# Moving a LayerNorm's sums and seven subtractions' operands to the vector engine, and cutting the last two norms into three parts

## The chip, the cores and the metric

The kernel runs on one core of one Trainium2 chip. The time is device microseconds of one launch; three runs of the kernel before gave 2405.48, 2411.17 and 2411.96 us, median 2411.17 us. The engines in the text are PE (TensorE, matrix products), DVE (VectorE), ACT (ScalarE), POOL (GpSimd) and SP (SyncE, which issues most DMAs).

## The reference, cut to what matters

One layer of a streaming encoder over 1088 tokens (1024 of a prompt, 64 of a running stream), model width 1024, feed-forward width 2816. Everything up to the mixed branch output `m` (a gated linear recurrence and a differential attention) is left out here; the change lies behind it:

```python
h   = layer_norm(ALPHA * x + m @ w_out, ln1_g, ln1_b)      # 1024 wide, over the features of one token
up  = h @ w_up                                             # 1024 x 5632: 2816 values and 2816 gates
c   = conv_b + sum(conv_w[j] * shifted(up, j) for j in range(3))
val, gate = split(c)
out = layer_norm(ALPHA * h + (silu(gate) * val) @ w_down, ln2_g, ln2_b)

def layer_norm(x, g, b):
    mu  = mean(x); var = mean(square(x - mu))
    return (x - mu) * rsqrt(var + 1e-5) * g + b
```

## The kernel before

Tokens lie along the free dimension and features along the 128 partitions, so `h` is eight tiles `z[0..7]` of 128 features. The 1088 tokens are four quarters of 272. Set c=0 holds quarters 0 and 2, set c=1 quarters 1 and 3; h=0 and h=1 name the two quarters of a set.

Every product is computed in three passes of single-pass float32 matmuls: each operand is split into a rounded part (hi, a cast on ACT) and the rest (lo, a subtraction on DVE), and hi*hi, hi*lo and lo*hi are summed in PSUM. `load_w` loads weights in tiles of 128x512 and splits them the same way (lines 82 and 83, names `whi` and `wlo`); `split_tokens` (lines 116 and 117) splits the activations, 128x1088 at a time.

`mix` ends with `out(0)`, the norms of set 0, and `out(1)`: the product with `w_out`, whose sums DVE moves to `z` (line 994). `layer_norm` takes the mean over 1024 features with eight full float32 matmuls with a matrix of 1/1024 (line 761, for the last set; two instructions each), subtracts it on DVE (line 773), squares on ACT (777 and 780), adds the squares up in two sums (781: for the last set one sum on POOL, one on DVE), turns the sums with small matmuls into a variance per token on the partitions (785), adds epsilon on DVE (792), takes the power -1/2 on POOL (793), spreads it again by a scaled identity (797, DVE) and a matmul (798), and scales and shifts (801 on DVE, 802 on ACT). `norm` then stores the quarter by two DMAs of ACT's queue and splits it.

`ffn` begins at line 1096. The first two of 22 feature pairs (f=0 and f=1) use `plain` (line 1051): a product of 24 matmuls for each quarter and each of two rows (value and gate). `norm(1, 0)` and `norm(1, 1)` stand between these. The other 20 pairs use `seven_products` (line 155), a scheme with 7 instead of 8 block products of each set, which needs besides b11, b21 and b22 the four combinations t1 to t4 of the blocks; `seven_tokens` (`sums(c)`) makes these by subtractions of 128x1088 in place (lines 125, 128, 130 and 133, on POOL) and splits them. The combinations of the weights are made on POOL as well (line 99). `conv` does the convolution of one pair, mostly on DVE.

Work on each engine is in order. The order is set at build time by a list scheduler: it simulates the engines and takes of what is ready the instruction that comes first in the program, or that was given a higher priority. Tiles come from pools of a fixed number of buffers; `mb` for instance has two, which the two parts of b12 of set 0 hold until the `plain` products of set 0 are done, and those of set 1 take after that.

The core of `ffn` before the seven-product loop:

```python
self.norm(1, 0)
plain(0, u0, 0, (0, 1))       # f, u, set, quarters: 2 rows x 2 quarters x 24 matmuls
self.norm(1, 1)
plain(1, u1, 0, (0, 1))
...
plain(0, u0, 1, (0,))
plain(1, u1, 1, (0,))
self.sums(0)
plain(1, u1, 1, (1,))
plain(0, u0, 1, (1,))
self.sums(1)
```

Of the kernel before, what the change touches and what calls it, by code (L numbers as in the profile page):

```python
# [10 lines left out]
F32 = mybir.dt.float32  # L11
# [3 lines left out]
ALU = mybir.AluOpType  # L15
# [5 lines left out]
P = 128  # L21
D = 1024
KT = D // P
# [6 lines left out]
EPS = 1e-5  # L30
# [7 lines left out]
QW = T // 4  # L38
# [12 lines left out]
class K:  # L51
# [67 lines left out]

    def seven_tokens(self, out, z, tile):  # L120

        V, G = self.nc.vector, self.nc.gpsimd
        b11, b21, b12, b22 = (z[n] for n in ("b11", "b21", "b12", "b22"))
        t1 = b11
        G.tensor_tensor(t1, b12, b11, ALU.subtract)
        self.split_tokens(out, "t1", t1, tile)
        t3 = b12
        G.tensor_tensor(t3, b22, b12, ALU.subtract)
        t2 = b22
        G.tensor_tensor(t2, b22, t1, ALU.subtract)  # L130
        self.split_tokens(out, "t2", t2, tile)
        t4 = b21
        G.tensor_tensor(t4, b21, t2, ALU.subtract)
        self.split_tokens(out, "t3", t3, tile)
        self.split_tokens(out, "t4", t4, tile)

    def seven_products(self, lanes, tmp):

# [609 lines left out]
        return [([t[:, c0:c0 + cw] for t in hs], [t[:, c0:c0 + cw] for t in ls]) for c0, cw in QUARTERS]  # L748


    def layer_norm(self, z, cw, og, ob, pp, lp, last=False):

        nc = self.nc
        V, S, G = nc.vector, nc.scalar, nc.gpsimd

        def lt(tag, bufs):
            return lp.tile([P, cw], F32, tag=tag, name=self.nm(tag), bufs=bufs)
        mean = pp.tile([P, 512], F32, tag="mm", name=self.nm("mean"))
        if last:
            for j in range(KT):  # L760
                nc.tensor.matmul(mean[:, :cw], self.ones_d, z[j], start=(j == 0), stop=(j == KT - 1))
        else:
            acc = lt("acc", 2)
            V.tensor_tensor(acc, z[0], z[1], ALU.add)
            for j in range(2, KT):
                V.tensor_tensor(acc, acc, z[j], ALU.add)
            nc.tensor.matmul(mean[:, :cw], self.ones_d, acc, start=True, stop=True)

        blocks = [(b, min(P, cw - b)) for b in range(0, cw, P)]
        var = pp.tile([P, 512], F32, tag="mm", name=self.nm("var"))  # L770
        sums = [None, None]
        for j in range(KT):
            V.tensor_tensor(z[j], z[j], mean[:, :cw], ALU.subtract)
            i = j % 2 if last else 0
            if sums[i] is None:
                sums[i] = lt("acc", 2)
                S.activation(sums[i], z[j], AF.Square)
                continue
            sq = lt("sq", 3)
            S.activation(sq, z[j], AF.Square)  # L780
            (V if i else G).tensor_tensor(sums[i], sums[i], sq, ALU.add)
        sums = [x for x in sums if x is not None]
        for i, (b, n) in enumerate(blocks):
            for j, x in enumerate(sums):
                nc.tensor.matmul(var[:n, i:i + 1], x[:, b:b + n], self.ones_d[:, 0:1], start=(j == 0),
                                 stop=(j == len(sums) - 1))
        rs = lp.tile([P, 2, 3], F32, tag="rs", name=self.nm("rs"), bufs=2)
        rb = pp.tile([P, 512], F32, tag="mm", name=self.nm("rb"))
        full = cw // P
        for n, i0, i1 in ((P, 0, full), (cw % P, full, len(blocks))):  # L790
            if i0 < i1:
                V.tensor_scalar(rs[:n, 0, i0:i1], var[:n, i0:i1], EPS, None, ALU.add)
                G.tensor_tensor(rs[:n, 1, i0:i1], rs[:n, 0, i0:i1], self.mhalf[:n].to_broadcast([n, i1 - i0]),
                                ALU.pow)
        for i, (b, n) in enumerate(blocks):
            dg = lp.tile([P, P], F32, tag="dg", name=self.nm("dg"), bufs=2)
            V.tensor_scalar(dg[:n, :n], self.ident[:n, :n], rs[:n, 1, i:i + 1], None, ALU.mult)
            nc.tensor.matmul(rb[:, b:b + n], self.ones_1[:n, :], dg[:n, :n], start=True, stop=True)
        for j in range(KT):
            g, b = self.par[:, og + j:og + j + 1], self.par[:, ob + j:ob + j + 1]  # L800
            V.scalar_tensor_tensor(z[j], z[j], g, rb[:, :cw], ALU.mult, ALU.mult)
            S.activation(z[j], z[j], AF.Identity, bias=b)
# [133 lines left out]
    def mix(self):  # L936
        tc, nc, a, o = self.tc, self.nc, self.a, self.o
        V, S, G = nc.vector, nc.scalar, nc.gpsimd
        mm, lnp = self.mm, self.lnp
# [3 lines left out]
        lp = ms.enter_context(tc.tile_pool(name="lp", bufs=2, **right))  # L943
# [7 lines left out]
        def m1t(name, dt=F32R):  # L951
            return m1.tile([P, 4, QW], dt, tag="mc", name=self.nm(name), bufs=16)
# [21 lines left out]
        def m2t(name, dt=F32R, tag="mc"):  # L974
            return m2.tile([P, 4, QW], dt, tag=tag, name=self.nm(name), bufs=12 if tag == "mc" else 2)
# [4 lines left out]
        lp = self.lx.enter_context(tc.tile_pool(name="ln", bufs=2, **right))  # L980
# [4 lines left out]
        def out(c):  # L985
            for j in range(KT):
                w = self.load_w(self.wcols(a["w_out"][0], j * P))
                for h, q in enumerate(pairs[c]):
                    c0 = q * QW
                    ps = self.proj_chunk(mm, w, [mh[q][k // 4][:, k % 4, :] for k in range(KT)],  # L990
                                         [ml[q][k // 4][:, k % 4, :] for k in range(KT)], QW)
                    xr = small("g")
                    nc.sync.dma_start(xr, self.s_x[j * P:(j + 1) * P, c0:c0 + QW])
                    V.scalar_tensor_tensor(zs[c][f"b{1 + j // 4}{1 + h}"][:, j % 4, :], xr, ALPHA, ps,
                                           ALU.mult, ALU.add)

        def norm(c, h):

            c0 = pairs[c][h] * QW
            names = [f"b{1 + i}{1 + h}" for i in range(2)]  # L1000
            z = [zs[c][n] for n in names]
            self.layer_norm([z[k // 4][:, k % 4, :] for k in range(KT)], QW, self.o_l1g, self.o_l1b, lnp, lp, c == 1)
            for i in range(2):
                S.dma_start(self.s_r.rearrange("(i k p) t -> i p k t", i=2, p=P)[i, :, :, c0:c0 + QW], z[i])
                self.split_tokens(self.xop[c], names[i], z[i],
                                  lambda n: m2t(n, tag="mb") if names[i] == "b12" else m1t(n))
# [4 lines left out]
        self.norm, self.sums = norm, sums  # L1011
        out(0)
        for h in range(2):
            norm(0, h)
        out(1)

    def ffn(self):
        tc, nc, a, o = self.tc, self.nc, self.a, self.o
        V, S, G = nc.vector, nc.scalar, nc.gpsimd
# [5 lines left out]
        mm, lnp = self.mm, self.lnp  # L1025
# [16 lines left out]
        def put(u, c):  # L1042
            def f(row, half):
                t0 = (2 * half + c) * QW
                for s0, s1, off in ((0, TP, 2), (TP, T, 4)):
                    b, e = max(s0, t0), min(s1, t0 + QW)
                    if b < e:
                        yield slice(b - t0, e - t0), u[:, row, b + off:e + off]
            return f

        def plain(f, u, c, halves, rows=(0, 1)):

            for row in rows:
                w = self.load_w(self.wcols(a["w_up"][0], (f + row * NF) * P))
                for h in halves:
                    x = self.xop[c][f"b1{1 + h}"] + self.xop[c][f"b2{1 + h}"]
                    ps = self.proj_chunk(mm, w, [k[0] for k in x], [k[1] for k in x], QW)
                    for sl, dst in put(u, c)(row, h):
                        S.copy(dst, ps[:, sl])
# [28 lines left out]


        u0, u1 = us = [new_u(f) for f in range(2)]  # L1090
        self.norm(1, 0)
        plain(0, u0, 0, (0, 1))
        self.norm(1, 1)
        plain(1, u1, 0, (0, 1))
        self.lx.close()
        cp = self.ux.enter_context(tc.tile_pool(name="upc", bufs=1, side="right", reuse_waits="tile"))
        plain(0, u0, 1, (0,))
        plain(1, u1, 1, (0,))
        self.sums(0)
        plain(1, u1, 1, (1,))  # L1100
# [24 lines left out]
        for ci, (c0, cw) in enumerate(DCH):  # L1125
# [16 lines left out]
            for j in range(KT):  # L1142
                ps = mm.tile([P, 512], F32, tag="mm", name=self.nm("mm"))
                for g0, gn in ((0, 8), (8, 8), (16, 6)):
                    src = wd[g0 * P:(g0 + gn) * P, j * P:(j + 1) * P].rearrange("(k p) c -> p k c", p=P)
                    w = self.load_w(src, gn)
                    for k in range(gn):
                        f = g0 + k
                        hi, lo = w[k]
                        for i, (l, r) in enumerate(((hi, ah), (hi, al), (lo, ah))):  # L1150
                            nc.tensor.matmul(ps[:, :cw], l, r[f][:, :cw], start=(f == 0 and i == 0),  # L1151
                                             stop=(f == NF - 1 and i == 2))
                hr = ft.tile([P, DW], F32, tag="hr", name=self.nm("hr"), bufs=2)
                nc.sync.dma_start(hr[:, :cw], self.s_r[j * P:(j + 1) * P, c0:c0 + cw])
                z = ft.tile([P, DW], F32, tag="z", name=self.nm("z2"), bufs=2)
# [6 lines left out]
            for i, (r, n) in enumerate(rows):  # L1162
# [3 lines left out]
                sq = ft.tile([P, D], F32, tag="sq", name=self.nm("sq"), bufs=1)  # L1166
# [7 lines left out]
                k = min(n, TP - t0)  # L1174
# [38 lines left out]
```

## Time and profile before

| what | value |
|---|---|
| median of 3 runs | 2411.17 us (2405.48 to 2411.96) |
| profiled execution, own time | 2406.6 us |
| its span in the trace | 2404.8 us |
| mean granted TensorE clock | 0.992 |
| PE busy | 2345.5 us, 98% |
| DVE busy | 1546.2 us, 64% |
| ACT busy | 1103.3 us, 46% |
| POOL busy | 549.1 us, 23% |

Times in the profile are microseconds from the start of the span. Busy time of an engine leaves out its waits. A timeline row gives start, duration, engine, line, operation, the tile written and the tiles read, how many instructions of the same kind follow one another, and in brackets how long the engine stood idle before it and what ended that. The granted clock is a share of full speed.

### The profile page before, as it was taken

The page shows a single profiled execution, that of the slowest core. Times are in us where ns is not written, and L with a number is a line of the kernel's source. Part 1 is how long each engine was busy: PE and PEld are TensorE (multiplying, and loading weights), DVE is VectorE, ACT ScalarE, POOL GpSimd, SP SyncE. Part 2 cuts the span into 40 slices and gives each one's busy share as a digit, 9 for nine tenths or more (in the row PEclk, how much of TensorE's full clock was granted, in tenths as well). Part 3 has the DMA queues.
Part 4 walks back from the last instruction along what each step waited for, and adds up shares of the span by engine and source line. Part 5 has one row for each costly group of instructions (what it writes and reads, how often), then busy time and mean ns, then how long its engine had stood idle before and what let it go on. Part 6 is the DMA issues. An engine that isn't in the chain of part 4 may idle for free.

```text
span 2404.8 us, 42987 instructions
## 1 busy us (share of the span) xinstructions
PE 2345.5 (98%) x16534; PEld 2289.3 (95%) x16534; DVE 1546.2 (64%) x2672; ACT 1103.3 (46%) x2134; POOL 549.1 (23%) x594
## 2 busy tenths in 40 slices
PE   8999999999999999999999999998999999989997
PEld 8999999999999999999999999998999999989997
DVE  3666665554666565565557565578978777766764
ACT  3444444443344444444447543245444444456664
POOL 2222222222521121121120000144544444200100
PEclk9999999999999999999999999998999999999999
DMA  4111111112622332332336674444332233298865
GB/s 128 39 40 47 42 44 49 40 35 65 200 81 79 108 90 73 98 99 74 96 92 199 200 243 136 131 140 125 104 94 82 85 94 95 84 268 252 241 202 150
DMA packets 404580, 273.02 MB, mean 114 GB/s; under 512 B 21803, under 2 KB 393927, under 8 KB 404374
## 3 DMA queue, kind: packets, MB, share of 16 engines
q1 hardware_dynamic: 399638, 265.52, 37.3%
q10 hardware_dynamic: 4224, 4.46, 0.6%
q8 instruction: 130, 2.13, 0.4%
q0 software_dynamic: 512, 0.29, 0.1%
q14 instruction: 76, 0.62, 0.1%
HBM read 199.65 MB, written 57.96 MB: 107 GB/s over the span
## 4 chain that ended last, share of the span: by engine, by line
PE 89%; DMA 3%; DVE 3%; ACT 2%; issue 1%; POOL 0%; SPq 0%; POOLq 0%; DVEq 0%; ACTq 0%
PE mm L182 46%; PE mm L155 18%; PE mm L1151 11%; PE s L645 3%; PE av L686 2%; PE wt L680 1%; PE lv L408 1%; PE nat L334 1%; DMA gb<-s_g 1%; PE o L491 1%; DVE wlo L83 1%; DMA ydl<-s_yd 1%; PE o L494 1%; PE avd L731 1%; PE bs L441 1%
## 5 line engine op out<-in xcount | busy, mean ns | idle before, releaser
L182 PE MATMUL mm<-x,whi 128*128 128x362 f32 (+1 forms) x3456 | 876.5, 333 | 5.0 <-ACT x L312 3.7
L182 PEld LDWEIGHTS mm<-x,whi 128*128 128x128 f32 x3456 | 611.7, 189 | 10.8 <-ACT x L312 4.4
L182 PE MATMUL mm<-x,wlo 128*128 128x362 f32 (+1 forms) x1728 | 573.2, 332 | 0.0
L83 DVE TENSOR_TENSOR wlo<-wraw,whi 128x512 fp32r<-128x512 f32 x516 | 377.0, 736 | 267.0 <-ACT whi L82 257.3
L82 ACT CAST whi<-wraw 128x512 fp32r<-128x512 f32 x516 | 308.5, 605 | 439.3 <-PE mm L182 211.5
L182 PEld LDWEIGHTS mm<-x,wlo 128*128 128x128 f32 x1728 | 326.7, 189 | 1.7 <-issue 1.0
L1151 PE MATMUL mm<-ah,whi 128*128 128x288 f32 (+1 forms) x688 | 200.3, 292 | 2.1 <-ACT ah L1135 2.1
L1151 PE MATMUL mm<-al,whi 128*128 128x288 f32 (+1 forms) x688 | 200.1, 291 | 1.5 <-DVE al L1136 1.5
L1151 PE MATMUL mm<-ah,wlo 128*128 128x288 f32 (+1 forms) x688 | 200.2, 292 | 0.0
L1151 PEld LDWEIGHTS mm<-ah,whi 128*128 128x128 f32 x688 | 131.2, 191 | 2.6 <-ACT ah L1135 2.4
L1151 PEld LDWEIGHTS mm<-al,whi 128*128 128x128 f32 x688 | 130.8, 190 | 1.9 <-DVE al L1136 1.9
L1151 PEld LDWEIGHTS mm<-ah,wlo 128*128 128x128 f32 x688 | 130.6, 190 | 1.0 <-DVE wlo L83 0.9
L536 POOL TENSOR_TENSOR rs<-rs,mhalf 128x4 f32<-128x4 f32 (+1 forms) x24 | 22.0, 919 | 372.7 <-DVE rs L535 372.7
L572 POOL TENSOR_TENSOR KL<-kT,B 64x512 fp32r<-64x512 f32 x32 | 49.2, 1539 | 218.1 <-DVE B L571 193.5
L82 ACT CAST whi<-wsum 128x512 fp32r<-128x512 f32 x80 | 49.6, 620 | 89.2 <-PE mm L155 84.2
L645 PE MATMUL s<-B,A 128*128 128x512 f32 (+3 forms) x384 | 87.7, 354 | 2.1 <-ACT E L666 1.6
L388 POOL TENSOR_TENSOR P<-X,k 128x544 f32<-128x544 f32 (+1 forms) x32 | 60.3, 1884 | 122.8 <-ACT X L382 68.7
L169 DVE TENSOR_TENSOR u<-mm,p 128x272 f32<-128x272 f32 (+2 forms) x160 | 55.1, 366 | 49.7 <-PE mm L155 49.7
L681 ACT COPY wT<-wt 128x512 f32<-128x512 f32 (+1 forms) x96 | 46.3, 482 | 80.1 <-PE wt L680 79.5
L99 POOL TENSOR_TENSOR wsum<-wraw,wraw 128x512 f32<-128x512 f32 x40 | 72.6, 1814 | 45.6 <-DVE wlo L83 45.5
L686 PE MATMUL av<-dvn,wT 128*128 128x128 f32 x576 | 80.0, 275 | 0.1
L1074 DVE SCALAR_TENSOR_TENSOR c<-u,par,c 128x1090 f32<-128x1090 f32 x44 | 78.4, 1782 | 0.3 <-ACT c L1071 0.3
(382 smaller groups left out, 5918.5 us busy)
## 6 DMA issues: line engine op xcount, KB each, us to landing
wraw<-w_down SPq DMA_DIRECT2D x160, 256.0 KB, 3.6
wraw<-w_in SPq DMA_DIRECT2D x144, 256.0 KB, 2.9
wraw<-w_up SPq DMA_DIRECT2D x124, 256.0 KB, 3.1
wraw<-w_br_hg SPq DMA_DIRECT2D x48, 256.0 KB, 4.1
s_act<-c SPq DMA_DIRECT2D x22, 512.0 KB, 3.1
A<-A SPq DMA_DIRECT2D x64, 128.0 KB, 2.6
wraw<-w_out SPq DMA_DIRECT2D x32, 256.0 KB, 2.9
araw<-s_act SPq DMA_DIRECT2D x44, 144.0 KB, 4.0
```

The source lines that it names most:

```text
L82: nc.scalar.copy(hi[:, :kn, :], raw[:, :kn, :])
L83: nc.vector.tensor_tensor(lo[:, :kn, :], raw[:, :kn, :], hi[:, :kn, :].bitcast(F32), ALU.subtract)
L99: G.tensor_tensor(t, x, y, op)
L155: nc.tensor.matmul(ps, l, r, start=(first and k == 0 and i == 0), stop=(k == 3 and i == 2), skip_group_check=not first)
L169: V.tensor_tensor(dst, ps[:, sl], d[other][:, sl], ALU.add)
L182: nc.tensor.matmul(ps[:, :cw], l, r[:, :cw], start=(k == 0 and i == 0), stop=(k == n - 1 and i == 2))
L388: G.tensor_tensor(pk, xv[:, :, :hb], blocks(k, B)[:, :, :hb], ALU.mult)
L572: G.tensor_tensor(kl[r], kT[r, sl], b[r, m, :].bitcast(F32), ALU.subtract)
L645: nc.tensor.matmul(dst[:, kc * 512:kc * 512 + kw], A[i // 2][:, p, m, qc], B[kc][:, m, :kw], start=(p == 0), stop=(p == 1))
L686: self.last_av = nc.tensor.matmul(av[:, i % n4, :], wT[:, kb, :], vn[:, kb, :], start=(kb == 0), stop=(kb == i))
L1074: V.scalar_tensor_tensor(t[:, :W - 2], u[:, i, 1:W - 1], par[:, self.o_w1 + j:self.o_w1 + j + 1], t[:, :W - 2], ALU.mult, ALU.add)
L1151: nc.tensor.matmul(ps[:, :cw], l, r[f][:, :cw], start=(f == 0 and i == 0), stop=(f == NF - 1 and i == 2))
```

## The change

1. `seven_tokens` makes t1 to t4 on DVE instead of POOL.
2. In the last set's norms all sums of squares are on DVE (before: alternating POOL and DVE). Norms of set 0 keep theirs on POOL.
3. The 272 columns are taken as three blocks of 128, the third (from column 144) overlapping the second, where before the third had 16. So epsilon and the power are one instruction each for all three, not two. `dg` has three buffers instead of two.
4. `layer_norm` and `norm` become generators with two stops: after the mean's matmuls, and after the variance's. `ffn` calls both last norms up to the first stop ahead of all `plain` products, and the other parts between single rows of these. The second norm's mean takes its PSUM bank from the pool `mm` of six.
5. The mean's matmuls (last set), the variance's, and all from epsilon to the spreading matmul get a priority 2000 instructions ahead of their place.

```diff
--- before.py
+++ after.py
@@ -119,20 +119,16 @@
 
     def seven_tokens(self, out, z, tile):
 
-        V, G = self.nc.vector, self.nc.gpsimd
+        V = self.nc.vector
         b11, b21, b12, b22 = (z[n] for n in ("b11", "b21", "b12", "b22"))
-        t1 = b11
-        G.tensor_tensor(t1, b12, b11, ALU.subtract)
-        self.split_tokens(out, "t1", t1, tile)
-        t3 = b12
-        G.tensor_tensor(t3, b22, b12, ALU.subtract)
-        t2 = b22
-        G.tensor_tensor(t2, b22, t1, ALU.subtract)
-        self.split_tokens(out, "t2", t2, tile)
-        t4 = b21
-        G.tensor_tensor(t4, b21, t2, ALU.subtract)
-        self.split_tokens(out, "t3", t3, tile)
-        self.split_tokens(out, "t4", t4, tile)
+        V.tensor_tensor(b11, b12, b11, ALU.subtract)
+        self.split_tokens(out, "t1", b11, tile)
+        V.tensor_tensor(b12, b22, b12, ALU.subtract)
+        V.tensor_tensor(b22, b22, b11, ALU.subtract)
+        self.split_tokens(out, "t2", b22, tile)
+        V.tensor_tensor(b21, b21, b22, ALU.subtract)
+        self.split_tokens(out, "t3", b12, tile)
+        self.split_tokens(out, "t4", b21, tile)
 
     def seven_products(self, lanes, tmp):
 
@@ -748,25 +744,31 @@
         return [([t[:, c0:c0 + cw] for t in hs], [t[:, c0:c0 + cw] for t in ls]) for c0, cw in QUARTERS]
 
 
-    def layer_norm(self, z, cw, og, ob, pp, lp, last=False):
+    def layer_norm(self, z, cw, og, ob, pp, lp, last=False, mp=None):
+
 
         nc = self.nc
         V, S, G = nc.vector, nc.scalar, nc.gpsimd
 
         def lt(tag, bufs):
             return lp.tile([P, cw], F32, tag=tag, name=self.nm(tag), bufs=bufs)
-        mean = pp.tile([P, 512], F32, tag="mm", name=self.nm("mean"))
+
+        ahead = 2000
+        mean = (mp or pp).tile([P, 512], F32, tag="mm", name=self.nm("mean"))
         if last:
-            for j in range(KT):
-                nc.tensor.matmul(mean[:, :cw], self.ones_d, z[j], start=(j == 0), stop=(j == KT - 1))
+            with self.tc.high_priority(offset=ahead):
+                for j in range(KT):
+                    nc.tensor.matmul(mean[:, :cw], self.ones_d, z[j], start=(j == 0), stop=(j == KT - 1))
         else:
             acc = lt("acc", 2)
             V.tensor_tensor(acc, z[0], z[1], ALU.add)
             for j in range(2, KT):
                 V.tensor_tensor(acc, acc, z[j], ALU.add)
             nc.tensor.matmul(mean[:, :cw], self.ones_d, acc, start=True, stop=True)
-
-        blocks = [(b, min(P, cw - b)) for b in range(0, cw, P)]
+        yield
+
+
+        starts = [*range(0, cw - P, P), cw - P]
         var = pp.tile([P, 512], F32, tag="mm", name=self.nm("var"))
         sums = [None, None]
         for j in range(KT):
@@ -778,24 +780,27 @@
                 continue
             sq = lt("sq", 3)
             S.activation(sq, z[j], AF.Square)
-            (V if i else G).tensor_tensor(sums[i], sums[i], sq, ALU.add)
+            (V if last else G).tensor_tensor(sums[i], sums[i], sq, ALU.add)
         sums = [x for x in sums if x is not None]
-        for i, (b, n) in enumerate(blocks):
-            for j, x in enumerate(sums):
-                nc.tensor.matmul(var[:n, i:i + 1], x[:, b:b + n], self.ones_d[:, 0:1], start=(j == 0),
-                                 stop=(j == len(sums) - 1))
-        rs = lp.tile([P, 2, 3], F32, tag="rs", name=self.nm("rs"), bufs=2)
-        rb = pp.tile([P, 512], F32, tag="mm", name=self.nm("rb"))
-        full = cw // P
-        for n, i0, i1 in ((P, 0, full), (cw % P, full, len(blocks))):
-            if i0 < i1:
-                V.tensor_scalar(rs[:n, 0, i0:i1], var[:n, i0:i1], EPS, None, ALU.add)
-                G.tensor_tensor(rs[:n, 1, i0:i1], rs[:n, 0, i0:i1], self.mhalf[:n].to_broadcast([n, i1 - i0]),
-                                ALU.pow)
-        for i, (b, n) in enumerate(blocks):
-            dg = lp.tile([P, P], F32, tag="dg", name=self.nm("dg"), bufs=2)
-            V.tensor_scalar(dg[:n, :n], self.ident[:n, :n], rs[:n, 1, i:i + 1], None, ALU.mult)
-            nc.tensor.matmul(rb[:, b:b + n], self.ones_1[:n, :], dg[:n, :n], start=True, stop=True)
+        nb = len(starts)
+        with self.tc.high_priority(offset=ahead):
+            for i, b in enumerate(starts):
+                for j, x in enumerate(sums):
+                    nc.tensor.matmul(var[:, i:i + 1], x[:, b:b + P], self.ones_d[:, 0:1], start=(j == 0),
+                                     stop=(j == len(sums) - 1))
+        yield
+        with self.tc.high_priority(offset=ahead):
+            rs = lp.tile([P, 2, nb], F32, tag="rs", name=self.nm("rs"), bufs=2)
+            rb = pp.tile([P, 512], F32, tag="mm", name=self.nm("rb"))
+            V.tensor_scalar(rs[:, 0], var[:, :nb], EPS, None, ALU.add)
+            G.tensor_tensor(rs[:, 1], rs[:, 0], self.mhalf.to_broadcast([P, nb]), ALU.pow)
+            done = 0
+            for i, b in enumerate(starts):
+                o = done - b
+                dg = lp.tile([P, P], F32, tag="dg", name=self.nm("dg"), bufs=3)
+                V.tensor_scalar(dg[:, o:], self.ident[:, o:], rs[:, 1, i:i + 1], None, ALU.mult)
+                nc.tensor.matmul(rb[:, done:b + P], self.ones_1, dg[:, o:], start=True, stop=True)
+                done = b + P
         for j in range(KT):
             g, b = self.par[:, og + j:og + j + 1], self.par[:, ob + j:ob + j + 1]
             V.scalar_tensor_tensor(z[j], z[j], g, rb[:, :cw], ALU.mult, ALU.mult)
@@ -999,7 +1004,8 @@
             c0 = pairs[c][h] * QW
             names = [f"b{1 + i}{1 + h}" for i in range(2)]
             z = [zs[c][n] for n in names]
-            self.layer_norm([z[k // 4][:, k % 4, :] for k in range(KT)], QW, self.o_l1g, self.o_l1b, lnp, lp, c == 1)
+            yield from self.layer_norm([z[k // 4][:, k % 4, :] for k in range(KT)], QW, self.o_l1g, self.o_l1b,
+                                       lnp, lp, c == 1, mm if c and h else None)
             for i in range(2):
                 S.dma_start(self.s_r.rearrange("(i k p) t -> i p k t", i=2, p=P)[i, :, :, c0:c0 + QW], z[i])
                 self.split_tokens(self.xop[c], names[i], z[i],
@@ -1011,7 +1017,8 @@
         self.norm, self.sums = norm, sums
         out(0)
         for h in range(2):
-            norm(0, h)
+            for _ in norm(0, h):
+                pass
         out(1)
 
     def ffn(self):
@@ -1088,13 +1095,21 @@
 
 
         u0, u1 = us = [new_u(f) for f in range(2)]
-        self.norm(1, 0)
-        plain(0, u0, 0, (0, 1))
-        self.norm(1, 1)
-        plain(1, u1, 0, (0, 1))
+        n0, n1 = self.norm(1, 0), self.norm(1, 1)
+        next(n0)
+        next(n1)
+        plain(0, u0, 0, (0, 1), (0,))
+        next(n0)
+        plain(0, u0, 0, (0, 1), (1,))
+        next(n0, None)
+        plain(1, u1, 0, (0, 1), (0,))
+        next(n1)
+        plain(1, u1, 0, (0, 1), (1,))
+        plain(0, u0, 1, (0,), (0,))
+        next(n1, None)
         self.lx.close()
         cp = self.ux.enter_context(tc.tile_pool(name="upc", bufs=1, side="right", reuse_waits="tile"))
-        plain(0, u0, 1, (0,))
+        plain(0, u0, 1, (0,), (1,))
         plain(1, u1, 1, (0,))
         self.sums(0)
         plain(1, u1, 1, (1,))
```

## Rows read from the trace of the kernel before

**Rows 1.** Windows: length, then busy time (count) by engine, clock, DMA share, GB/s

```profile
1580.00:1590.00 10.00, 10.00 (x83) 9.81 (x81) 6.13 (x14) 2.30 (x4) 2.90 (x2) 1.00 0.79 233
1621.40:1626.80 5.40, 5.40 (x32) 5.40 (x33) 1.40 (x6) 1.68 (x4) 1.26 (x2) 0.68 0.23 67
1626.80:1652.20 25.40, 25.40 (x192) 24.38 (x190) 16.64 (x36) 15.23 (x34) 4.56 (x5) 1.00 0.45 133
1661.00:1666.30 5.30, 5.29 (x25) 5.29 (x26) 5.30 (x4) 2.42 (x4) 3.92 (x2) 0.54 0.52 147
1678.50:1683.46 4.96, 4.96 (x24) 4.96 (x25) 4.96 (x6) 1.66 (x3) 4.96 (x6) 0.56 0.55 159
1609.70:1683.46 73.76, 62.25 (x427) 59.88 (x427) 60.06 (x86) 42.09 (x85) 33.09 (x24) 0.88 0.40 116
1683.46:1704.60 21.14, 21.14 (x170) 21.14 (x170) 20.79 (x26) 11.67 (x19) 12.47 (x16) 1.00 0.29 90
```

**Rows 2.** Timeline of PE: the last norms' two means, and waits before 1683.5

```profile
1604.46 3.83 PE L761 MATMUL mean<-zb,ones_d 128*128 128x272 f32 x16
1620.04 1.31 PE L785 MATMUL var<-ones_d,acc 128*128 128x1 f32 x12 [2.85 <-POOL acc L781]
1627.12 3.14 PE L761 MATMUL mean<-zb,ones_d 128*128 128x272 f32 x13
1658.84 1.12 PE L182 MATMUL mm<-b12h,whi 128*128 128x272 f32 x3 [1.75 <-ACT b12h L116]
1661.01 0.59 PE L182 MATMUL mm<-b12l,whi 128*128 128x272 f32 x1 [1.05 <-DVE b12l L117]
1671.59 0.39 PE L182 MATMUL mm<-b22h,wlo 128*128 128x272 f32 x1 [0.76 <-DVE wlo L83]
1678.46 0.60 PE L182 MATMUL mm<-b12h,wlo 128*128 128x272 f32 x1 [5.10 <-DVE wlo L83]
```

**Rows 3.** Timeline of DVE, the same stretch

```profile
1609.73 0.42 DVE L994 SCALAR_TENSOR_TENSOR zb<-g,mm 128x272 f32<-128x272 f32 x1
1610.08 1.28 DVE L117 TENSOR_TENSOR t2l<-zb,t2h 128x1088 fp32r<-128x1088 f32 x1
1614.47 2.86 DVE L773 TENSOR_TENSOR zb<-zb,mean 128x272 f32<-128x272 f32 x8
1622.37 0.48 DVE L797 TENSOR_SCALAR dg<-ident,rs 128x128 f32<-128x128 f32 x2 [0.77 <-POOL rs L793]
1639.06 0.44 DVE L781 TENSOR_TENSOR acc<-acc,sq 128x272 f32<-128x272 f32 x1
1657.00 2.76 DVE L83 TENSOR_TENSOR wlo<-wraw,whi 128x512 fp32r<-128x512 f32 x1 [0.15 <-ACT whi L82]
1660.88 0.68 DVE L83 TENSOR_TENSOR wlo<-wraw,whi 128x512 fp32r<-128x512 f32 x1
1661.48 3.60 DVE L117 TENSOR_TENSOR b22l<-zb,b22h 128x1088 fp32r<-128x1088 f32 x1
1665.00 4.83 DVE L117 TENSOR_TENSOR t1l<-zb,t1h 128x1088 fp32r<-128x1088 f32 x2
1669.76 4.71 DVE L83 TENSOR_TENSOR wlo<-wraw,whi 128x512 fp32r<-128x512 f32 x2
1674.39 2.34 DVE L117 TENSOR_TENSOR t2l<-zb,t2h 128x1088 fp32r<-128x1088 f32 x1
1676.66 1.75 DVE L83 TENSOR_TENSOR wlo<-wraw,whi 128x512 fp32r<-128x512 f32 x1
```

**Rows 4.** Timeline of POOL, the same stretch

```profile
1616.14 0.77 POOL L781 TENSOR_TENSOR acc<-acc,sq 128x272 f32<-128x272 f32 x1 [6.88 <-ACT sq L780]
1655.71 3.50 POOL L125 TENSOR_TENSOR zb<-zb,zb 128x1088 f32<-128x1088 f32 x1 [9.44 <-ACT zb L802]
1668.64 2.34 POOL L99 TENSOR_TENSOR wsum<-wraw,wraw 128x512 f32<-128x512 f32 x1
1670.94 2.98 POOL L133 TENSOR_TENSOR zb<-zb,zb 128x1088 f32<-128x1088 f32 x1
```

## The prediction, made before the changed kernel was run

> **What bounds the kernel now.** I read four views: the busy table, the windows around the change, PE's timeline there, and then the timelines of the engines that its waits name. The busy table has PE at 98% of the span, so time is won only where PE waits or runs at a low clock. The windows show one such place. From the last product of the second set with w_out (1609.7) to the first seven-product (1683.46) PE is busy 62.25 of 73.76 us at a mean granted clock of 0.88; just behind, 170 matmuls take 21.14 us at 1.00, or 0.1244 us each [rows 1]. The reader is to see two losses in the first stretch: gaps, and windows of 0.54 to 0.68 behind them.
>
> How much is lost there: PE's own work is 16 blocks of 24 matmuls, 384 x 0.1244 = 47.8 us; the second norm's mean, 16 instructions like those of 3.83 us; two variances of 1.31 us [rows 2]; two spreading steps of the same kind, of half as many instructions, some 0.65 each. Sum 47.8 + 3.8 + 2.6 + 1.3 = 55.5 us; 73.76 - 55.5 = 18.2 us are lost. The brackets of PE's timeline name 11.5 of them: 2.85 for the sums of squares of the first norm, 1.75 and 1.05 for the parts of b12, 0.76 and 5.10 for a weight's lo part [rows 2]. Slow clock behind three of these gaps: 32 + 25 + 24 = 81 instructions in 5.40 + 5.30 + 4.96 = 15.66 us instead of 81 x 0.1244 = 10.1, so 5.6 us [rows 1]. That leaves 1.1 us unnamed. The change lies in this stretch, so 18 us is its ceiling.
>
> Why DVE was late: from 1657 to 1678.4 it was busy without a break, but with instructions that last far over their size. A wlo takes 0.68 alone and 2.76 at 1657.00; a split takes 1.28 (t2l at 1610.08) and 3.60 at 1661.48. The six groups from 1657.00 to 1676.66 exceed their undisturbed durations by 2.08 + 2.32 + 2.27 + 3.35 + 1.06 + 1.07 = 12.2 us [rows 3]. Beside each of them a POOL subtraction or sum runs: the wlo of 1657.00 ends at 1659.76, the POOL instruction of 1655.71 at 1659.21 [rows 3, 4]. Some 3.3 us of the excess lie beside the weight sums of line 99, which stay (1668.64 and two more); 8.9 us lie beside the instructions that leave POOL.
>
> **The change part by part.** *t1 to t4 on DVE.* Set 1 costs DVE 4 x 1.28 = 5.1 us more, priced by the split of equal size, and gives back 8.9 [rows 3]; the bounds of one such subtraction are 1.28 and, blocked by POOL, 3.60. The step itself becomes shorter for t1, from 3.50 to 1.28 us [rows 3, 4]. Set 0's four run during the product before, where PE has work (10.00 of 10.00 us busy at clock 1.00 [rows 1]); I count nothing, and if they delay the evacuations there, at worst 5.1 us.
>
> *Sums of squares on DVE.* Six adds at 0.44 on DVE instead of six at 0.77 on POOL [rows 3, 4], so DVE +2.6 us, while the chain of a pair loses a hop. In all DVE has 60.06 - 8.9 + 5.1 + 2.6 = 58.9 us of work in the stretch; before, it stood idle for 73.76 - 60.06 = 13.7. It fits beside PE's 55.5 only because splits of t2 to t4 and the convolutions of f=0 and 1 may slip into the products, where DVE has 20.79 of 21.14 us [rows 1] but PE does not wait for it.
>
> *Three blocks of 128.* One epsilon and one power less for each norm, and the third scaled identity no longer waits for a buffer: some tenths, beside PE's rows. Counted as nothing; bounds 0 to 0.8 us gained for each of the two norms (the wait for the power was 0.77 [rows 3]).
>
> *The second mean ahead.* Before it ran at 1627.12, though the last of its data, the evacuation of 1609.73, was there at 1610.2 [rows 2, 3]. Its place is now before all plain products, 15 us earlier or so. From its start to b12's lo part (PE continues at 1661.01) it took 34 us [rows 2]; begun at 1609.7 the same chain ends at 1644. PE comes to b12 after 12 blocks, 288 x 0.1244 = 35.8, plus 3.8 + 2.6 + 1.3 for the norms' steps: 1653. The two `mb` buffers of b12 come free after eight blocks, at about 1640, which is early enough to split. So both waits for b12 and the slow clock behind them go: 1.75 + 1.05 + (5.30 - 25 x 0.1244 = 2.2) = 5.0 us. With 9 us in hand I take all of it; bounds 0 to 5.0.
>
> *The weights behind it.* 0.76 + 5.10 + (4.96 - 24 x 0.1244 = 2.0) = 7.9 us. DVE's queue there is shortened by 8.9, and b12's and b22's splits move ahead into its idle time, but the four subtractions come in and the sums of line 99 stay. I take 5.5 us, leaving one gap of about 1.5 with its slow clock; bounds 0 and 7.9.
>
> *The first variance.* 2.85 us, and 5.40 - 32 x 0.1244 = 1.4 us of slow clock. The mean was done at 1608.3, but DVE began to subtract at 1614.47, because splits of set 0 stood in its queue (t2l at 1610.08 and two more) [rows 2, 3]. The edit does not remove these, and adds subtractions in front of them, while the adds get quicker and the second mean with a row of plain (3.8 + 6.0 us) covers PE. I take 2.3 of 4.2; bounds 4.2 gained and 9.3 lost (the slower rival below).
>
> *Added waits.* The second mean is queued behind the last evacuation; behind it on PE stand the plain rows. Every step with raised priority stands in PE's in-order queue where the build's simulation has it ready: when DVE is later, all plain matmuls wait. I take 1.0 us lost; bounds 0 and 3. The mean's bank from the pool of six leaves five, with 3 us of matmuls each: nothing. Raised priorities in set 0's norms: they already come before the product around them in the program, and PE shows no gap there [rows 1]; nothing, at worst a wait of 1.3 us (0.77 + 0.48, the power and the identity [rows 3]) for each. DMAs and weight loads are as many as before; single rows load in the same order, and SP's queue is moved past nothing but the two stores of a norm, which are on ACT's queue.
>
> Sum: 5.0 + 5.5 + 2.3 - 1.0 = 11.8 us. The profiled execution took 2406.6 us (span 2404.8), so 2394.8 on its scale; it lies 4.6 us under the median, from which the same gain gives 2399.4. I put the time between them, **2397 us**.
>
> **The rivals.** *DVE becomes the bound of the stretch.* For it: 58.9 us of work against 55.5 of PE's, and POOL's weight sums, now started early because POOL is free, may meet the new DVE subtractions. Each such meeting has cost between 1.06 and 2.32 us [rows 3]; four at the mean of 1.7 add 6.8. Then the stretch is 58.9 + 6.8 = 65.7 us plus some 3.6 of slow clock behind gaps, 69.3: gain 4.5, time 2402 to 2407. Against it: much of DVE's work there has no early reader. The Trainium skill, SBUF — State Buffer, section "Who interferes with whom", says that a DVE instruction with two SBUF inputs and a GpSimd instruction that reads SBUF exclude each other, and that whichever starts second waits for the whole of the first; the wlo that ends just behind POOL's instruction agrees. By that rule the lock does not go with the subtractions; it stays wherever line 99 runs.
>
> *PE waits at the raised steps (slower).* Place: the first variance, if the simulation has it ready directly behind the second mean, at 1613.5, while DVE's queue still holds set 0's four subtractions and three splits, 7 x 1.28 = 9.0 us, ahead of subtracting the mean (2.86) and the adds (2.6) [rows 3]. Data come at 1608.3 + 14.5 = 1622.8: a wait of 9.3. Then 1.3 for the first spreading step, 5.5 for the second variance, 1.3 for the second spread, and two spells of slow clock of 2 us: 21.4. Of the 18.2 lost now, the 12.9 around b12 and the weights shrink to 2.4, 1.1 stay: 21.4 + 2.4 + 1.1 - 18.2 = 6.7 us slower, 2413 to 2418. It decides once the waits at these four steps pass 14.7 us with their slow clock. For it: they lasted 4.2 for one step already. Against: what PE waited for at that step was POOL's sum [rows 2], which goes.
>
> *The order hardly changes.* The scheduler may have placed the steps by readiness already; then only the 8.9 us of blocking go, and the weights' gap of 7.9 shrinks by some 5: 2402 to 2406.
>
> *All goes:* 18 us, 2388 to 2393.
>
> **How the numbers follow.** Chances: forecast (8 to 16 us gained) 0.53, all goes 0.06, DVE bound 0.24, order unchanged 0.05, slower 0.12. Within 0.3%, 7.2 us, a change of this kernel can hardly be told from none. So faster 0.60 (forecast, all goes, a little of the others), same 0.28, slower 0.12. The range from 2388 to 2412 holds all but the slower case and the very best.
>
> **What would show it.** Right: no subtraction of 128x1088 on POOL, wlo of the stretch at 0.68 except beside line 99; the second mean before the plain rows; no wait of PE on b12; the stretch 61 to 63 us long at a clock over 0.94. Wrong: a PE wait of several us at the variance or the spreading step, or at a weight's lo part with DVE busy throughout; or the same gain in the stretch given back among the first seven-products, whose convolutions free the two u buffers.

## The result: 2388.84 us, 0.8% faster, where 2397 us were forecast

The changed kernel takes 2388.84 us (median of 6 runs, 2386.66 to 2393.93) against 2410.78 us before (6 runs, 2403.55 to 2414.50); the ratio is 0.9919, 95% interval 0.990 to 0.9938, so 15 to 24 us less. The profiled execution took 2388.5 us, 18.1 less than before's. The forecast was 2397 us, 11.8 us of gain. What moved to DVE are the last norms' sums of squares and the four subtractions of each set that make the operands t1 to t4 of the seven products; DVE is nevertheless busy 6.0 us less.

| | before | after |
|---|---|---|
| span | 2404.8 us | 2386.6 us |
| mean granted clock | 0.992 | 0.995 |
| DVE busy | 1546.2 us | 1540.2 us |
| POOL busy | 549.1 us | 520.7 us |

The windows of the kernel after, for the stretch that [rows 1] show of before (columns as there); the last plain matmul starts at 1663.5, the first seven-product at 1661.9:

```profile
1609.10:1661.90 52.80, 52.80 (x425) 52.72 (x425) 46.63 (x88) 37.70 (x81) 8.26 (x8) 1.00 0.49 148
...
1661.90:1682.90 21.00, 19.63 (x157) 19.41 (x156) 20.14 (x20) 13.14 (x22) 15.24 (x17) 1.00 0.42 127
1682.90:1703.90 21.00, 20.46 (x162) 20.17 (x162) 20.76 (x28) 9.86 (x15) 9.11 (x15) 1.00 0.27 84
1703.90:1724.90 21.00, 21.00 (x170) 21.00 (x169) 20.09 (x31) 9.95 (x16) 13.04 (x23) 1.00 0.38 123
```

425 PE instructions now take 52.80 us, all of it busy at clock 1.00, where 427 took 73.76 at 0.88 [rows 1]. The two counts are nearly the same work: 2 instructions of the second mean now lie inside instead of 16, and 12 of the product with w_out instead of none. The two windows behind it are new: PE is idle 1.37 and 0.54 us, with DVE nearly full (20.14 and 20.76 of 21.00 us). PE's timeline after, to be held against [rows 2]:

```profile
1590.05 3.00 PE L761 MATMUL mean<-zb,ones_d 128*128 128x272 f32 x12
...
1603.88 3.37 PE L761 MATMUL mean<-zb,ones_d 128*128 128x272 f32 x14
...
1615.72 0.62 PE L761 MATMUL mean<-zb,ones_d 128*128 128x272 f32 x2
...
1619.27 1.17 PE L789 MATMUL var<-ones_d,acc 128*128 128x1 f32 x10
...
1678.23 0.40 PE L151 MATMUL mm<-t3h,whi 128*128 128x272 f32 x1 [1.37 <-DVE p L158]
...
1698.65 0.39 PE L151 MATMUL mm<-t3h,whi 128*128 128x272 f32 x1 [0.54 <-DVE p L158]
```

None of the five waits of before is left. The means no longer run in two blocks; their matmuls are scattered from 1590 on through the product before. DVE's and POOL's timelines after ([rows 3] and [rows 4] answer to them):

```profile
1609.13 2.87 DVE L775 TENSOR_TENSOR zb<-zb,mean 128x272 f32<-128x272 f32 x8 [0.90 <-PE mean L761]
...
1640.63 1.29 DVE L117 TENSOR_TENSOR b12l<-zb,b12h 128x1088 fp32r<-128x1088 f32 x1 [0.86 <-ACT b12h L116]
...
1646.65 1.29 DVE L127 TENSOR_TENSOR zb<-zb,zb 128x1088 f32<-128x1088 f32 x1
...
1654.47 2.50 DVE L83 TENSOR_TENSOR wlo<-wraw,whi 128x512 fp32r<-128x512 f32 x4
...
1673.22 1.43 DVE L83 TENSOR_TENSOR wlo<-wsum,whi 128x512 fp32r<-128x512 f32 x1
...
1674.92 1.65 DVE L83 TENSOR_TENSOR wlo<-wraw,whi 128x512 fp32r<-128x512 f32 x1
1676.49 1.34 DVE L1083 SCALAR_TENSOR_TENSOR c<-u,par,c 128x1090 f32<-128x1090 f32 x1
1677.75 0.78 DVE L158 TENSOR_TENSOR p<-mm,p 128x272 f32<-128x272 f32 x2
```

```profile
1655.57 3.85 POOL L1075 COPY cst<-u 128x2 f32<-128x2 f32 x1 [25.54 <-ACT u L1066]
1659.36 0.18 POOL L1076 COPY cst<-u 128x2 f32<-128x2 f32 x1
...
1671.87 2.23 POOL L99 TENSOR_TENSOR wsum<-wsum,wraw 128x512 f32<-128x512 f32 x1
1674.72 1.30 POOL L99 TENSOR_TENSOR wsum<-wraw,wraw 128x512 f32<-128x512 f32 x1 [0.63 <-DVE wlo L83]
```

Until line 99 starts (1659.76) DVE's lo parts take 0.6 to 0.7 us each and a subtraction 1.29; b12's lo part is there at 1642, not 1661. What remains of the blocking stands where line 99 runs, and PE's wait of 1.37 us is for a move (p) queued behind two such lo parts and a step of the convolution.

### The profile page after: what moved, and what is told of

It is laid out like the page before. It is cut to its first block, busy times and chain, and to the rows that moved or that the text cites. A ratio compares the mean times of both kernels' runs of the same rounds, so it can differ in the third digit from the quotient of the medians.

```text
span 2386.6 us, 42975 instructions
## 1 busy us (share of the span) xinstructions
PE 2337.9 (98%) x16534; PEld 2283.0 (96%) x16534; DVE 1540.2 (65%) x2682; ACT 1103.7 (46%) x2134; POOL 520.7 (22%) x576
## 4 chain that ended last, share of the span: by engine, by line
PE 89%; DMA 3%; DVE 3%; ACT 2%; issue 1%; POOL 0%; SPq 0%; POOLq 0%; DVEq 0%; ACTq 0%
PE mm L178 47%; PE mm L151 17%; PE mm L1166 9%; PE s L641 3%; PE av L682 2%; PE wt L676 1%; PE lv L404 1%; PE nat L330 1%; DMA gb<-s_g 1%; PE o L487 1%; DMA ydl<-s_yd 1%; DMA wraw<-w_down 1%; PE o L490 1%; PE avd L727 1%; DVE wlo L83 1%
## 5 line engine op out<-in xcount | busy, mean ns | idle before, releaser
L83 DVE TENSOR_TENSOR wlo<-wraw,whi 128x512 fp32r<-128x512 f32 x516 | 364.7, 712 | 263.6 <-ACT whi L82 257.1
```

What stands on the lines that cost most here:

```text
L83: nc.vector.tensor_tensor(lo[:, :kn, :], raw[:, :kn, :], hi[:, :kn, :].bitcast(F32), ALU.subtract)
```

## The experiments

Eleven kernels ran, each timed in several runs against the kernel before. They were timed on three later occasions, each beside its own runs of the kernel before (medians 2409.48, 2409.37 and 2409.98 us); the changed kernel itself was timed only on the first, so a difference of medians between it and the others also holds what differs between occasions. Their profiled executions start the changed stretch at different times, though until some 6 us before R the four engines do the same in the same order. So besides the medians I count from R, one matmul that all kernels have: the last one of the mean of set 0's second norm (line 767; 1569.2 us in the trace before, 1568.9 after). The table gives in us from R the start of the last plain matmul, the first matmul of the product with w_down (behind all seven-products) and the end of the span, each good to 0.1 us.

| kernel | median us | ratio to before, interval | plain ends | w_down begins | span ends |
|---|---|---|---|---|---|
| before | 2410.78 | | 114.0 | 539.3 | 835.6 |
| changed | 2388.84 | 0.9919 [0.9900, 0.9938] | 94.6 | 521.9 | 817.7 |
| tokens_on_pool | 2399.16 | 0.9959 [0.9945, 0.9972] | 99.3 | 527.5 | 823.9 |
| norms_whole | 2398.28 | 0.9962 [0.9949, 0.9974] | 103.4 | 529.5 | 826.5 |
| only_tokens_on_dve | 2401.59 | 0.9968 [0.9957, 0.9979] | 99.0 | 532.0 | 827.9 |
| all_but_pool_to_dve | 2395.11 | 0.9944 [0.9931, 0.9956] | 99.5 | 526.7 | 822.1 |
| no_priority | 2395.01 | 0.9942 [0.9929, 0.9956] | 96.9 | 527.6 | 823.1 |
| mean_no_priority | 2396.23 | 0.9946 [0.9934, 0.9959] | 94.6 | 525.9 | 822.1 |
| sums_alternating | 2393.17 | 0.9933 [0.9920, 0.9945] | 94.6 | 521.4 | 817.0 |
| conv_late | 2392.23 | 0.9928 [0.9916, 0.9941] | 94.6 | 521.8 | 818.2 |
| pool_beside | 2396.95 | 0.9953 [0.9938, 0.9968] | 100.3 | 529.0 | 826.3 |
| first_weight_sums_on_dve | 2388.72 | 0.9918 [0.9903, 0.9932] | 94.6 | 519.9 | 815.8 |
| sums_pool_weights_dve | 2392.08 | 0.9934 [0.9919, 0.9948] | 94.6 | 519.9 | 816.8 |

From the start of w_down to the end every kernel needs between 295.4 and 297.3 us, though the change does not touch that part; one difference there is a spell of granted clock 0.5 (1.2 GHz) just behind w_down's first matmuls, 3.4 us long in some traces and 6.8 in others. A difference of the last column of 1 or 2 us counts only if the column of w_down has it too.

**tokens_on_pool** undoes the subtractions on DVE.

```diff
-        V.tensor_tensor(b11, b12, b11, ALU.subtract)
+        G.tensor_tensor(t1, b12, b11, ALU.subtract)
...
```

> The changed kernel with the subtractions for t1 to t4 back on POOL; all else stays changed. Theory A (blocking): most of the gain is DVE no longer held up beside POOL's subtractions. Then DVE's instructions beside them grow by some 9 us in the stretch again, PE waits again for a weight's lo part before the products, with slow clock behind it, and the time is 8 to 12 us over the changed kernel's, 2397 to 2401. Theory B (order): most of the gain is that both means and the second norm come earlier. Then DVE has enough idle time to absorb the blocking, and the time is 0 to 4 us over, 2389 to 2393.

By the median 10.3 us over the changed kernel, from R 6.2. Theory A's price by the median, between A and B from R. The wait of A is back, on lo parts before the products, beside one wait for p in them (total, times, longest):

```profile
PE mm L182 <- DVE wlo L83: 3.0, 2, 2.4
PE mm L155 <- DVE p L162: 1.3, 1, 1.3
```

**norms_whole** undoes the cutting of the norms.

```diff
+        for _ in self.norm(1, 0):
+            pass
+        plain(0, u0, 0, (0, 1))
+        for _ in self.norm(1, 1):
+            pass
+        plain(1, u1, 0, (0, 1))
...
```

> The changed kernel with both last norms called in one piece, at their old places between the plain products, and the second mean back in the pool of two; subtractions and sums stay on DVE, raised priorities stay. Theory A (blocking): 0 to 4 us over the changed kernel, 2389 to 2393, PE hardly waits. Theory B (order): the second mean runs after half of set 0's products again, PE waits at the first variance and for b12, and the time is 8 to 12 us over, 2397 to 2401.

9.4 us over by the median, 8.8 from R: theory B's price, with its wait for b12 (the wait at the first variance, which it named too, did not come):

```profile
PE mm L178 <- ACT b12h L116: 3.5, 1, 3.5
PE mm L178 <- DVE wlo L83: 2.3, 2, 1.3
```

**only_tokens_on_dve** is the kernel before with this one edit (the diff's first part alone).

> The kernel before with one edit alone: the subtractions for t1 to t4 on DVE. Theory A (blocking): over half of the 22 us comes, 2396 to 2400. Theory B (order): 0 to 8 us of gain, 2403 to 2411. If both add up, this gain and the one of the run with all but this edit make 22 us.

7.7 us from R and about as much by the ratio (0.9968 of 2409.5: 7.7). The plain rows end 15.0 us earlier, but 7.7 of them are lost again by the start of the product with w_down: 433.0 us lie between these points, 425.3 before. The median, 2401.59, lies between the two theories' ranges, the gain in theory B's. PE still waits for b12 in the plain rows (line 178), and now in the first seven-products (line 151) on DVE and ACT; the wait at the first variance is gone. The longest waits:

```profile
PE mm L178 <- ACT b12h L116: 2.1, 1, 2.1
PE mm L151 <- DVE wlo L83: 1.9, 1, 1.9
PE mm L151 <- DVE p L158: 1.2, 1, 1.2
PE mm L151 <- ACT u L1055: 1.0, 1, 1.0
```

**all_but_pool_to_dve** keeps everything else: the subtractions and half the sums go back to POOL.

> The changed kernel with the subtractions and the alternating half of the sums of squares back on POOL, so that only the cut norms, the three blocks of 128 and the priorities are changed. Theory A (blocking): 2 to 8 us of gain against the kernel before, 2403 to 2409. Theory B (order): 14 us or more, at most 2397.

13.5 us from R, by the ratio 13.5 too (0.9944 of 2409.5). That is the better half, theory B, though not quite the 14 us asked for. With sums_alternating below, four kernels form a square, from R: neither 835.6, tokens alone 827.9 (7.7 less), cut norms with priorities alone 822.1 (13.5), both 817.0 (18.6). Neither theory alone holds; the two parts nearly add up from R, 21.2 against 18.6. By the medians, each against before on its occasion, they overlap more: 7.9 and 14.4 alone, 16.2 together. The three blocks of 128 and the mean's other PSUM pool were not tried by themselves; the blocks stand in every kernel with cut norms, and in norms_whole, where they did not save the time.

**no_priority** and **mean_no_priority** set the priority's offset to 0 for all steps, and for the means alone.

```diff
-        ahead = 2000
+        ahead = 0
```

> The changed kernel with the raised priority set to none, so that the means, the variances and the steps up to the spreading matmul are ordered by their place in the program. Theory P: priority is what brings the second mean into the product before the plain ones and the short steps ahead of other DVE work; then the second mean runs behind that product, PE waits for b12 or a weight again, and the time is 4 to 10 us over the changed kernel's. Rival: the program's new order alone does it, 0 to 2 us over, 2389 to 2391.

> The changed kernel with the raised priority taken from the means' matmuls alone. Theory P: the second mean is later than 1616, all steps of the second norm with it, but b12 was ready some 14 us ahead of its use, so 0 to 2 us over the changed kernel, 2389 to 2391; what the priority gives must then come from the short steps. Rival: the means' place is what counts, and the time is as without any priority, 4 to 10 us over.

From R 5.4 and 4.4 us over, by the medians 6.2 and 7.4. Against conv_late, which turned out to be the changed kernel once more and was timed beside these two, the medians are only 2.8 and 4.0 over. Either way nearly all that priority gives comes from the means' matmuls; the rival of the second run is right, if at the lower end of its price, and my theory in it wrong. PE's work before the products hardly changes (the plain rows end at 96.9 and 94.6). The means run only behind the set-1 product, b12 comes later, and the loss falls into the first seven-products. PE, DVE, and PE's waits in the kernel without priority:

```profile
1604.70 5.67 PE L761 MATMUL mean<-zb,ones_d 128*128 128x272 f32 x24
```

```profile
1612.03 5.65 DVE L775 TENSOR_TENSOR zb<-zb,mean 128x272 f32<-128x272 f32 x16 [0.56 <-PE mean L761]
...
1647.22 1.29 DVE L117 TENSOR_TENSOR b12l<-zb,b12h 128x1088 fp32r<-128x1088 f32 x1 [0.64 <-ACT b12h L116]
```

```profile
PE mm L151 <- DVE p L158: 3.5, 3, 2.3
PE mm L151 <- ACT whi L82: 1.6, 1, 1.6
```

DVE subtracts the first mean 1.7 us later from R, and the second directly behind it (x16), ahead of the first norm's adds; in the changed kernel (x8) all six of these come between. b12's lo part starts 77.1 us after R (1647.22, R at 1570.1), 71.7 in the changed kernel: DVE's chain is 5.4 us later, and so is the end of the span.

**sums_alternating** undoes the move of the sums of squares.

```diff
-            (V if last else G).tensor_tensor(sums[i], sums[i], sq, ALU.add)
+            (V if i else G).tensor_tensor(sums[i], sums[i], sq, ALU.add)
```

> The changed kernel with half of the last norms' sums of squares back on POOL, the subtractions staying on DVE. Theory A (blocking): POOL's six adds of 0.77 us stand beside DVE's work in the norms, PE waits up to 2 us at the variances, 1 to 4 us over the changed kernel, 2390 to 2393. Rival (DVE is short of time, and the adds cost it 2.6 us): 0 to 3 us under it, 2386 to 2389. The two runs with the subtractions on POOL point to the rival, since there the adds on POOL were the faster ones.

From R 0.7 us under the changed kernel; with the subtractions on POOL the same comparison (all_but_pool_to_dve against tokens_on_pool) gives 1.8 under. The medians point the other way, 4.3 over with overlapping intervals, but 0.9 over conv_late, timed on the same occasion. This part of the change gains nothing that could be shown.

**conv_late** put the convolution of f=1 behind the first seven-products.

```diff
-        for f in range(2):
-            conv(f, us[f])
+        conv(0, us[0])
...
+            if f == 2:
+                conv(1, u1)
```

> The changed kernel with the convolution of f=1 placed behind the first seven-products instead of before them, to test what gives back some 2 us in the first two rounds of these. Theory D (DVE's backlog: the convolutions of f=0 and 1 stand ahead of the moves that free PSUM): the waits of 1.4 and 0.5 us for p go, and the time is 1 to 3 us under the changed kernel's, 2386 to 2388. Rival: the later convolution keeps its buffer of u, the wait moves to the second round, and the time is the same or up to 3 us over.

The scheduler made of it the same instructions in the same order on every engine. So it tested nothing of either theory, but it is the changed kernel a second time: the same work gave medians of 2388.84 and 2392.23 us on two occasions, and 817.7 and 818.2 us from R. On the second occasion the gain over before is 17.1 us (2409.37, ratio 0.9928), close to the count from R and not to the 22 us of the first.

**pool_beside** adds POOL work that nobody waits for to the changed kernel; the order on the other engines is the same.

```diff
+        xb = self.xop[1]["b12"]
+        for i in range(16):
+            x = xb[i % 4][0].bitcast(F32)
+            G.tensor_tensor(self.beside, x, x, ALU.subtract)
         self.sums(1)
...
```

> The changed kernel with 16 useless POOL subtractions of 128x272 added (two inputs in SBUF, about as much work as four of 128x1088), which nothing waits for and which start once b12 of set 1 is split, near 1642; every other engine has the same instructions in the same order. Theory A (blocking alone, without any later operand): DVE's subtractions and lo parts beside them last longer by 5 to 9 us in sum, DVE falls behind, PE waits for a weight's lo part before or in the first products, and the time is 3 to 8 us over the changed kernel's. Rival (what hurt before was that t1 to t4 came late, and DVE has time to spare): 0 to 2 us over.

8.6 us over from R, 8.1 by the medians: theory A, just above its range. Of the 8.6, 5.7 are there when the plain rows end and 7.1 at the start of w_down; the last 1.5 lie behind it, where kernels with equal work differ as much. t1 to t4 are made on DVE here as in the changed kernel. The weight sums of line 99 also start 7.1 us later from R (98.0 against 90.9), but POOL stood idle for 0.70 and 0.91 us between the added work and them. DVE beside it, POOL, and PE's waits:

```profile
1646.53 1.73 DVE L126 TENSOR_TENSOR zb<-zb,zb 128x1088 f32<-128x1088 f32 x1
...
1664.34 3.37 DVE L83 TENSOR_TENSOR wlo<-wraw,whi 128x512 fp32r<-128x512 f32 x4
```

```profile
1644.32 21.65 POOL L1121 TENSOR_TENSOR beside<-b12h 128x272 f32<-128x272 f32 x16 [10.66 <-DMA s_r<-zb]
```

```profile
PE mm L178 <- DVE wlo L83: 3.3, 3, 2.1
PE mm L151 <- DVE p L158: 2.3, 2, 1.7
PE mm L151 <- DVE wlo L83: 0.8, 1, 0.8
```

Each DVE subtraction of 1.29 us takes 1.72 or 1.73 while POOL runs, a lo part of 0.69 takes 1.12, and POOL's own take 21.65 / 16 = 1.35 us instead of 0.77 [rows 4]. In order of their starts one instruction of DVE and one of POOL alternate throughout, 16 of each: the two engines take turns. The Trainium skill, SBUF — State Buffer, section "Who interferes with whom", says that a DVE instruction with two SBUF inputs contends with a GpSimd instruction that reads SBUF, for a shared port pair under an exclusive lock. That both engines lose time here agrees; but a DVE instruction lost only 0.43 or 0.44 us to a POOL instruction that takes 0.77 alone, so a wait for the whole of it is not seen.

**first_weight_sums_on_dve** takes line 99 of the first two rounds to DVE.

```diff
-            G.tensor_tensor(t, x, y, op)
+            (nc.vector if c1 < 4 * P else G).tensor_tensor(t, x, y, op)
```

> The changed kernel with the sums of weights of f=2 and f=3 on DVE instead of POOL, to test what gives back some 2 us in the first seven-products. Theory A (DVE is held up beside line 99 there): the lo parts of 1.24 to 1.77 us come back to 0.68, eight sums of 0.65 us are added, PE's waits of 1.4 and 0.5 us shrink, and the end lies 1 to 2 us earlier. Rival (DVE has no time left there, whatever POOL does): the same waits or longer ones, 0 to 3 us later.

1.9 us under from R, 2.0 already at the start of w_down, and PE's waits in the products fall from 1.9 to 0.4 us. DVE's lo parts there, 1.24 to 1.77 us in the changed kernel, take 0.7 again, with the sums added to DVE's queue: what the change gave back was blocking beside line 99, not a lack of time on DVE. The medians (2388.72 against 2388.84) do not tell the two apart. PE's waits there:

```profile
PE mm L151 <- DVE p L158: 0.4, 1, 0.4
```

**sums_pool_weights_dve** joins this edit to the one of sums_alternating.

> Both: the sums of weights of f=2 and f=3 on DVE, and the last norms' sums of squares alternating between POOL and DVE as before the change. In the trace the alternating sums alone ended 0.7 us earlier than the changed kernel, counted from the last norm of set 0. If both help, the end lies 2 to 3 us earlier than the changed kernel's; if not, within 1 us of the better one.

816.8 from R, within 1 us of the better one, and the same 519.9 at the start of w_down: the edits do not add up. No kernel tried has a median more than 0.12 us under the changed one's.

## Why the prediction was right in direction and too small

The place, the ceiling's nature and both mechanisms held: the gain lies in the stretch between the product with w_out and the seven-products. The size was off, 11.8 us against 17.9 from R (and 22 by the medians of the first occasion, 17 by those of the second, with conv_late). So the forecast, 8 to 16 us, did not come: what came is the rival *All goes*, 18 us and 2388 to 2393, to which I gave 0.06. That 2388.84 lies in the range from 2388 to 2412, by 0.84 us, owes as much to the range's width as to the sum. The signs named for a right forecast came in the main (two instructions of the second mean still lie among the plain rows), but the stretch was shorter than the 61 to 63 us named there.

- *Ceiling.* 18.2 us was short by some 1.6. I let the stretch begin at 1609.7, but PE had begun the plain rows at 1607.9, and 13 of the 384 matmuls that I counted inside had started before. From R the plain rows end 19.4 us earlier.
- *The second mean ahead and the waits for b12 (5.0).* Right: gone. Undoing the cut brought 3.8 us of such waits and cost 8.8.
- *The weights behind it (5.5 of 7.9).* Mis-sized: all of it went. I left a gap for the blocking of line 99, but those sums now start at 1659.8, when the plain rows' lo parts are done. I had not foreseen that on POOL four small copies stand ahead of them, of which the first started at 1655.57 and took 3.85 us; that all of the term went is in part luck.
- *The first variance (2.3 of 4.2).* Mis-sized: all of it went. The splits that stood ahead of the subtraction came earlier, beside PE's work (t2's lo part at 35.5 us from R, 40.8 before). Either part of the change by itself removes this wait: it stands neither in only_tokens_on_dve nor in all_but_pool_to_dve.
- *Raised priorities (1.0 lost).* This step failed, in sign. I priced the risk that PE waits at a step placed too early and saw no gain. No such wait occurred, and the means' priority is worth 4.4 us from R (4.0 by the medians of one occasion): their matmuls run inside the product before, DVE starts the first norm earlier and takes its adds ahead of the second norm's subtraction.
- *Given back.* Named as a way to be wrong and not priced: 2.0 us of the 19.4 are lost in the first two rounds of the products (427.3 us from the last plain matmul to w_down, 425.3 before).
- *t1 to t4 on DVE.* The balance of 5.1 us of work against 8.9 of blocking was of the right kind; pool_beside shows that blocking without later subtractions costs 7.1 us up to the start of w_down.
- *Sums of squares.* I counted a shorter chain. It brings nothing measurable, or costs about 1 us.

Of the rivals, the DVE-bound one has the cause right and the place wrong: DVE did not bound the stretch (46.63 of 52.80 us busy), but in the first seven-products, where it is full, a later DVE chain came back as PE time in the runs that had one (7.7 us with the subtractions alone, 4 without the means' priority). The slower rival did not occur: no wait at a raised step in any run with them. Nor did the unchanged order: the cut norms and priorities alone bring 13.5 us.

## What to carry to other kernels

When an elementwise step leaves POOL for DVE, count the time that DVE loses beside it, not only the step's own duration; here, by the prediction's estimate, 8.9 us of that stood against 5.1 of added work. An engine that is full behind a transition makes its earlier idle time valuable: look for what lets it start sooner, such as a small matmul that may run inside the product before, and follow the gain to the end of the kernel, since part of it can come back as waits some rounds later. Comparing profiles from a common instruction ahead of the change to one just behind it separated effects of about 2 us that medians with 3 us between two takes of the same order could not; and a kernel should be timed beside the ones it is compared with.

## What was not expected of the hardware

A POOL copy of 128x2 took 3.85 us at 1655.57, while DVE ran lo parts and a split without a break from 1654.47 to 1659.37, and the next copies took 0.18 us each when DVE stood idle. In the kernel without priority the same copy took 6.53 us, beside eight instructions of DVE in a row, and ended 0.05 us behind the last of them. The turns seen in pool_beside are thus not the rule: there one instruction of each engine alternated, here one small POOL instruction waited through several of DVE's. Which of the two happens was not tried.
